# The recurrence's gates and the attention's scores as plain float32 products of 64 partitions

## The chip, the cores and the metric

One program on one NeuronCore of a Trainium2 chip. The metric is the device time of one execution in microseconds (us). The kernel before takes 618.59 us (median of three runs, 617.87 to 619.34); the execution that was profiled took 616.12 us.

## The reference, cut to what matters

One layer of a hybrid backbone over 256 latent tokens and 256 context tokens of width 1024: a conv branch, an attention branch of 8 heads of 64, a recurrence of 8 blocks of 64 in two directions, then a mixture of 16 experts of which each token takes two. The two places that the change touches:

```python
def _block_diag(x, w, bias):                      # the recurrence's gates, 8 blocks of 64 x 64
    xb = x.reshape(bsz, length, RNN_BLOCKS, RNN_BLOCK_W)
    return jnp.einsum("blnk,nkj->blnj", xb, w).reshape(bsz, length, D_RNN) + bias

r = jax.nn.sigmoid(_block_diag(uf, wa, ba))
i = jax.nn.sigmoid(_block_diag(uf, wx, bx))
...
s_loc = jnp.einsum("bqhd,brkhd->bhqrk", qr, kb) * scale    # 64 dims of one head
s_ctx = jnp.einsum("bqhd,bchd->bhqc", qr, kc) * scale
p = jax.nn.softmax(jnp.concatenate([s_loc, s_ctx], axis=-1), axis=-1)
```

## The kernel before

Channels lie on partitions, 128 at a time, tokens along the free axis. Most matrix products are made of three float32r products of a high and a low part (`mm3`, L68 to L70, `gps` and others in the profile): a weight block arrives by DMA in a `raw` tile, ScalarE writes its high part `w` (L73), VectorE the low part (L74), and 24 matmuls of 256 columns use it. `split` (L72) does the same to an operand. This stream of weight blocks runs from 21 us to 362 us: the keys, the conv inputs (54 us on), the recurrence's inputs `rxps` (85 us on), the values, the queries, `rgps`, 24 gate blocks `gps` with 12 branch blocks `bps` between them (177 to 334 us), and the output `ops`. Then the experts run (374 us on), in float32, with weights that DMAs bring.

Beside the stream run generators: the conv's taps and norm in one queue, `rnn(0)`, `rnn(1)` and `attention()` in the other. Each `yield a, b` says how many us of TensorE and of VectorE the step just written takes, and `fill` takes steps from the queues behind each weight block until VectorE's sum has caught up with TensorE's (ScalarE is not in the account). Tile's scheduler then orders each engine's instructions by its own estimate, mostly as they were written.

`rnn(h)` has four units, a pair of 64-channel blocks `b` in a direction `d`. A unit makes `u` (L679, L686), then two full float32 products of 128 partitions, 128 rows out and 512 columns, `pa` (L688) and `px` (L689): their weights `rnnw` hold two 64 x 64 blocks on the diagonal and zeros elsewhere. ScalarE makes `r` of `pa` (L690) and `g` of `px` (L691), then L693 to L695 and VectorE L696 and L697.

`attention()` takes pairs of heads, `b`. The normed keys and queries `qkn` are split into high and low parts: `kz` for the keys of both heads, `qz` for the queries, where each head has a copy of its own with zeros in the other head's 64 partitions (memsets L788 and L789). A score block `sps` of one head and 128 queries is three float32r products of 128 partitions and 512 columns (L804 to L806). Softmax and `values` follow (L808 to L836). `big` has 35 tiles of 512 KB named pieces, which all of these and the first expert weights share; PSUM has four banks for `ax_bank` and four for `mm_bank`.

## Time and profile before

| | us |
|---|---|
| median of three runs (lowest, highest) | 618.59 (617.87, 619.34) |
| profiled execution | 616.12 |
| its span, first to last instruction | 614.3 |
| TensorE busy | 580.2 (94%) |
| VectorE busy | 349.1 (57%) |
| ScalarE busy | 259.8 (42%) |
| GpSimd busy | 19.4 (3%) |
| bytes moved by DMA | 170.65 MB, mean 278 GB/s |

Times in the rows are us from the first instruction, unless they are marked ns. PE is TensorE, PEld its weight loads, DVE VectorE, ACT ScalarE, SP the queue that issues most DMAs. A float32 product shows as two matmul instructions, a float32r one as one. A matmul's end is modelled, so the distance from one start to the next says more than its duration. A share of busy time is a mean over stages that have different limits.

### The profile page before, as it was taken

What the parts mean: (1) busy time and instruction counts of PE and PEld (TensorE: products, weight loads), DVE (VectorE), ACT (ScalarE), POOL (GpSimd) and SP (SyncE); (2) the same over time, 40 slices, a digit from 0 to 9 for tenths busy, and PEclk for the clock granted to TensorE, in tenths of its full rate; (3) what the DMA queues carried; (4) which work ended last, traced back from release to release, by engine and by line L of the source; (5) the groups of instructions that cost most, each with busy time, mean ns of one, the idle gap of its engine ahead of it and who ended that gap; (6) DMA issues with size and microseconds to landing.
All of it is one profiled execution on the core that took longest, in us unless ns stands there. A gap on an engine that the chain in (4) does not pass through costs nothing. (4 is left out here: it accounts for less than half of the span.)

```text
span 614.3 us, 10619 instructions
## 1 busy us (share of the span) xinstructions
PE 580.2 (94%) x4127; PEld 408.1 (66%) x4127; DVE 349.1 (57%) x797; ACT 259.8 (42%) x456; POOL 19.4 (3%) x42
## 2 busy tenths in 40 slices
PE   1899999999999899999999988999999999999986
PEld 0789888778788778888899975335445334454454
DVE  4667899999758968988469554121240314132303
ACT  4345446654598765877545624203012111130101
POOL 0000000000000000103112010000000000000000
PEclk9999999999999999999999999999999999999999
DMA  8983874446853463759969776999999999969961
GB/s 256 367 339 114 310 259 154 137 141 193 278 212 103 138 241 103 236 176 356 313 211 379 283 245 226 388 360 406 402 393 407 407 408 409 398 226 409 409 248 68
DMA packets 51825, 170.65 MB, mean 278 GB/s; under 512 B 5664, under 2 KB 10016, under 8 KB 51744
## 3 DMA queue, kind: packets, MB, share of 16 engines
q1 hardware_dynamic: 46704, 151.26, 67.2%
q0 software_dynamic: 5040, 18.35, 8.6%
q8 instruction: 46, 0.75, 0.5%
q14 instruction: 35, 0.29, 0.1%
HBM read 168.54 MB, written 1.05 MB: 276 GB/s over the span
## 5 line engine op out<-in xcount | busy, mean ns | idle before, releaser
L1162 PE MATMUL ph<-ew,xg 128*64 128x512 f32 (+1 forms) x576 | 115.6, 548 | 3.5 <-PEq L1318 2.8
L73 ACT ACTIVATE w<-raw 128x1024 fp32r<-128x1024 f32 x68 | 71.8, 1056 | 65.6 <-PE gps L69 11.6
L74 DVE TENSOR_TENSOR w<-raw,w 128x1024 fp32r<-128x1024 f32 x68 | 82.9, 1219 | 21.5 <-ACT w L73 20.8
L1162 PEld LDWEIGHTS ph<-ew,xg 128*64 128x64 f32 x576 | 41.5, 137 | 66.0 <-issue 58.3
L70 PE MATMUL gps<-h,w 128*128 128x256 f32 x192 | 55.2, 288 | 1.2 <-DVE w L74 1.2
L68 PE MATMUL gps<-h,w 128*128 128x256 f32 x192 | 56.0, 291 | 0.4 <-DVE y L934 0.4
L69 PE MATMUL gps<-h,w 128*128 128x256 f32 x192 | 54.5, 284 | 0.0
L593 DVE SCALAR_TENSOR_TENSOR cacc<-up,vc,cacc 128x243 f32<-128x243 f32 (+14 forms) x120 | 52.1, 472 | 1.4 <-ACT cacc L585 0.7
L1171 DVE SCALAR_TENSOR_TENSOR he<-sl,gsl,ph 128x256 f32<-128x256 f32 x16 | 7.1, 477 | 77.5 <-PE ph L1162 76.2
L1183 PE MATMUL py<-ew,heT 128*64 128x512 f32 x224 | 49.6, 595 | 1.2 <-ACT heT L1178 0.8
L74 DVE TENSOR_TENSOR ys<-py,ys 128x512 fp32r<-128x512 f32 (+1 forms) x18 | 11.4, 633 | 58.0 <-ACT ys L73 58.0
L68 PEld LDWEIGHTS gps<-h,w 128*128 128x128 f32 x192 | 36.6, 191 | 4.2 <-issue 2.6
L70 PEld LDWEIGHTS gps<-h,w 128*128 128x128 f32 x192 | 36.7, 191 | 2.8 <-issue 1.5
L69 PEld LDWEIGHTS gps<-h,w 128*128 128x128 f32 x192 | 36.7, 191 | 0.9 <-issue 0.7
L1183 PEld LDWEIGHTS py<-ew,heT 128*64 128x64 f32 x224 | 15.5, 137 | 30.8 <-issue 26.0
L1201 DVE SCALAR_TENSOR_TENSOR xl<-scp,g,xl 128x256 f32<-128x256 f32 x72 | 29.2, 475 | 7.5 <-PE scp L1197 7.5
L1167 ACT ACTIVATE sl<-ph 128x512 f32<-128x512 f32 (+1 forms) x9 | 5.0, 550 | 63.1 <-PE ph L1162 40.4
L73 ACT ACTIVATE ys<-py 128x512 fp32r<-128x512 f32 (+1 forms) x18 | 9.9, 550 | 50.5 <-PE py L1183 36.6
L114 POOL DMA_DIRECT2D ew<-in_w_exp x31 | 16.6, 537 | 321.1 <-ACT pp L813 248.8
L1119 ACT ACTIVATE xg<-gps,b2m 128x256 f32<-128x256 f32 x32 | 13.4, 471 | 22.7 <-PE gps L1115 21.8
L349 PE MATMUL mps<-ma,cs 128*32 128x256 f32 (+1 forms) x160 | 10.1, 397 | 13.2 <-DMA ma<-in_mod_a 13.1
L1197 PEld LDWEIGHTS scp<-oT,ys 128*128 128x128 f32 x128 | 15.7, 188 | 6.7 <-issue 5.2
(358 smaller groups left out, 1310.0 us busy)
## 6 DMA issues: line engine op xcount, KB each, us to landing
ew<-in_w_exp SPq DMA_DIRECT2D x161, 512.0 KB, 10.2
raw<-in_w_in SPq DMA_DIRECT2D x40, 512.0 KB, 4.4
ew<-in_w_exp POOLq DMA_DIRECT2D x31, 512.0 KB, 7.3
raw<-in_mod_b SPq DMA_DIRECT2D x28, 512.0 KB, 4.1
ma<-in_mod_a SPq DMA_DIRECT2D x12, 512.0 KB, 10.0
raw<-in_w_br SPq DMA_DIRECT2D x12, 512.0 KB, 4.0
raw<-in_w_out SPq DMA_DIRECT2D x8, 512.0 KB, 7.5
ma<-in_mod_a SPq DMA_DIRECT2D x8, 256.0 KB, 6.7
```

The lines of the kernel that those rows point to most:

```text
L68: pe.matmul(ps, wh, xh, start=start, stop=False, skip_group_check=True)
L69: pe.matmul(ps, wh, xl_, start=False, stop=False, skip_group_check=True)
L70: return pe.matmul(ps, wl, xh, start=False, stop=stop, skip_group_check=True)
L73: act.activation(hi, src, AF.Copy)
L74: dve.tensor_tensor(lo, src, r32(hi), op=ALU.subtract)
L114: queue.dma_start(t, w_exp[6 * p + 2 * i + s, :, 1024 * q:1024 * q + 1024])
L593: dve.scalar_tensor_tensor(cacc[:, b, i0:i1], up[:, b, i0 + o:i1 + o], half_d[:, b * 31 + j:b * 31 + j + 1], cacc[:, b, i0:i1], op0=ALU.mu ...
L1119: act.activation(place(k0 + j), ps[:, j, :], AF.Identity, bias=b2m[:, k0 + j:k0 + j + 1])
L1162: pe.matmul(ph[64 * s:64 * s + 64, cols], xg(k)[:, c:c + 64], w[:, at], start=k == 0 and not h, stop=k == KD - 1, skip_group_check=True)
L1183: pe.matmul(py[q][64 * s:64 * s + 64, :], heT[f // 2][:, f % 2, 64 * s:64 * s + 64], ew[p][2][f][s][:, q * 512:q * 512 + 512], start=f == ...
L1197: pe.matmul(ps[:, j, :], rows_(i, m), toks(m), start=(j == 0 and i == 0), stop=i == parts - 1, skip_group_check=True)
L1201: dve.scalar_tensor_tensor(xl[:, m, :], ps[:, j, :], g2[:, m:m + 1], xl[:, m, :], op0=ALU.mult, op1=ALU.add)
```

## The change

The gates: the two blocks of a unit become two float32 products of 64 partitions each, on partitions 0 to 63 and 64 to 127, each with 128 rows out, of which the first 64 are the one gate and the others the other gate; they go to two banks. The weights lose the zeros and take one piece and one DMA where there were two. ScalarE makes each of `r` and `g` in two instructions of 64 partitions, as the halves lie in two banks. The scores: a pair of heads is two float32 products of 64 partitions, straight from `qkn`, for the same 128 queries, into two banks. `qz` and `kz`, their memsets and splits go, and with them four pieces. A pair of heads is walked by query tile and then head; the planner's costs of the steps are other ones.

```diff
--- before.py
+++ after.py
@@ -660,9 +660,8 @@
     dve.tensor_scalar(ch, ch, -4.0, None, op0=ALU.mult)
     calm.close()
 
-    rnnw = [cut(piece(name="rnnw"), 0, [8, 128]) for _ in range(2)]
-    for d in range(2):
-        load(rnnw[d], rnn_w[:, 8 * d:8 * d + 8, :])
+    rnnw = cut(piece(name="rnnw"), 0, [8, 128])
+    load(rnnw, rnn_w)
     rxp = [cut(piece(name="rxp"), 0, [2, 2, T]) for _ in range(2)]
 
     def rnn(h):
@@ -684,12 +683,16 @@
                 else:
                     out_, in_ = uc[:, :, :T - o], src[:, :, o:]
                 dve.scalar_tensor_tensor(out_, in_, wj, out_, op0=ALU.mult, op1=ALU.add)
-            pa, px = ax_bank(name="pa"), ax_bank(name="px")
-            pe.matmul(pa, rnnw[d][:, 2 * h + b, :], u, start=True, stop=True)
-            pe.matmul(px, rnnw[d][:, 4 + 2 * h + b, :], u, start=True, stop=True)
-            act.activation(r, pa, AF.Tanh, bias=half_r[:, i:i + 1], scale=0.5)
-            act.activation(g, px, AF.Tanh, bias=half_r[:, 8 + i:9 + i], scale=0.5)
-            yield 1.7, 2.0
+
+            pab = [ax_bank(name="pab") for _ in range(2)]
+            for j in range(2):
+                c = slice(64 * j, 64 * j + 64)
+                pe.matmul(pab[j], rnnw[c, 4 * d + 2 * h + b, :], u[c], start=True, stop=True)
+            for o, x, n_ in ((0, r, i), (64, g, 8 + i)):
+                for j in range(2):
+                    c = slice(64 * j, 64 * j + 64)
+                    act.activation(x[c], pab[j][o:o + 64, :], AF.Tanh, bias=half_r[c, n_:n_ + 1], scale=0.5)
+            yield 1.1, 2.0
             act.activation(th, r, AF.Tanh, bias=ch[:, i:i + 1], scale=ch[:, i:i + 1])
             act.activation(r, r, AF.Exp, bias=ch[:, i:i + 1], scale=ch[:, i:i + 1])
             last = act.activation(a2, r, AF.Square)
@@ -780,30 +783,22 @@
             turned.append(tp.rearrange("p t (b c) -> p t b c", b=4)[:, :, :, :2])
         hrstd = rsqrt(turned, 48, 1.0 / HD).rearrange("p (t h) -> p t h", t=6)
         yield 0, 2.5
-        qz = []
-        for i in range(2):
-            t = piece(F32R, "qz")
-            H, L = cut(t, 0, [2, T]), cut(t, 512, [2, T])
-            for x in (H, L):
-                dve.memset(r32(x[64:128, 0, :]), 0.0)
-                dve.memset(r32(x[0:64, 1, :]), 0.0)
-            qz.append((H, L))
-        kz = [piece(F32R, "kz") for _ in range(2)]
         pp = [cut(piece(name="pp"), 0, [2, 512]) for _ in range(2)]
         pts = [cut(piece(name="pt"), 0, [4, T]) for _ in range(4)]
         att_out.extend(cut(piece(F32R, "att"), 0, [4, T]) for _ in range(2))
         oH, oL = att_out
-        yield 0, 1.1
         behind = []
 
-        def scores(b, hh, t):
-            ps = ax_bank(name="sps")
-            q = slice(t * 128, t * 128 + 128)
-            qH, qL = qz[b % 2]
-            kH, kL = kz[b % 2][:, :512], kz[b % 2][:, 512:]
-            pe.matmul(ps, qH[:, hh, q], kH, start=True, stop=False)
-            pe.matmul(ps, qH[:, hh, q], kL, start=False, stop=False)
-            pe.matmul(ps, qL[:, hh, q], kH, start=False, stop=True)
+        def scores(b, t):
+
+            ps = [ax_bank(name="sps") for _ in range(2)]
+            q = 512 + t * 128
+            for hh in range(2):
+                x = qkn[b % 2][64 * hh:64 * hh + 64]
+                pe.matmul(ps[hh], x[:, q:q + 128], x[:, :512], start=True, stop=True)
+            return ps
+
+        def softmax(b, hh, t, ps):
             bias = rpb[b][:, hh, 2 - 2 * t:6 - 2 * t, :].rearrange("p a b -> p (a b)")
             dve.tensor_tensor(ps[:, :T], ps[:, :T], bias, op=ALU.add)
             nm = work.tile([128, 1], F32, tag="nm", name="nm", bufs=4)
@@ -845,24 +840,19 @@
                 pe.transpose(psk[:, t * 128:t * 128 + 128], hx[:, t, :], ident)
             kn = qkn[b % 2][:, :512]
             dve.scalar_tensor_tensor(kn, kb[b], v("kg"), psk, op0=ALU.mult, op1=ALU.mult)
-            kH, kL = kz[b % 2][:, :512], kz[b % 2][:, 512:]
-            split(kH, kL, kn)
-            yield 0.5, 2.3
+            yield 0.5, 1.0
             psq = ax_bank((128, T), "psq")
             for t in range(2):
                 pe.transpose(psq[:, t * 128:t * 128 + 128], hx[:, 4 + t, :], ident)
             qn = qkn[b % 2][:, 512:512 + T]
             dve.scalar_tensor_tensor(qn, qb[:, b, :], qg8, psq, op0=ALU.mult, op1=ALU.mult)
-            qH, qL = qz[b % 2]
-            for hh in range(2):
-                s = slice(64 * hh, 64 * hh + 64)
-                split(qH[s, hh, :], qL[s, hh, :], qn[s, :])
-            yield 0.3, 1.2
+            yield 0.3, 0.5
             pt = pts[2 * (b % 2):2 * (b % 2) + 2]
-            for hh in range(2):
-                for t in range(2):
-                    behind.append((b, hh, t, scores(b, hh, t), pt))
-                    yield 0.7, 1.2
+            for t in range(2):
+                ps = scores(b, t)
+                for hh in range(2):
+                    behind.append((b, hh, t, softmax(b, hh, t, ps[hh]), pt))
+                    yield 1.0 * (1 - hh), 1.2
                     if len(behind) > DEEP:
                         values(*behind.pop(0))
                         yield 0.9, 0.6
@@ -1484,12 +1474,11 @@
     for br in (0, 2, 1):
         order += [CG + br * 8 + m for m in range(8)]
     d["w_in"] = C(np.stack([blk(b).reshape(128, 1024) for b in order]))
-    rw = np.zeros((128, 2, 2, 4, 128), np.float32)
+    rw = np.empty((2, 64, 2, 4, 2, 64), np.float32)
     for gi, a in enumerate((f(rnn_wa)[0], f(rnn_wx)[0])):
-        for n in range(8):
-            s = (n % 2) * 64
-            rw[s:s + 64, :, gi, n // 2, s:s + 64] = a[:, n].transpose(1, 0, 2)
-    d["rnn_w"] = C(rw.reshape(128, 16, 128))
+
+        rw[:, :, :, :, gi] = a.reshape(2, 4, 2, 64, 64).transpose(2, 3, 0, 1, 4)
+    d["rnn_w"] = C(rw.reshape(128, 8, 128))
     col = np.arange(64)
     start = np.clip(col - 8, 0, 48)
     inside = (col[None, :] >= start[:, None]) & (col[None, :] < start[:, None] + 16)
```

## Rows read from the trace of the kernel before

**Rows 1.** The page's first part: busy time, share of the span, instructions

```profile
PE 580.2 (94%) x4127; PEld 408.1 (66%) x4127; DVE 349.1 (57%) x797; ACT 259.8 (42%) x456; POOL 19.4 (3%) x42
```

**Rows 2.** Windows by stage: length, then busy us (instructions) of each engine, clock, DMA

```profile
98.00:133.00 35.00, 35.00 (x207) 26.20 (x204) 34.26 (x69) 21.30 (x30) 0.00 (x0) 1.00 0.44 142
...
165.00:211.00 46.00, 44.53 (x331) 37.70 (x331) 36.43 (x73) 40.72 (x63) 0.00 (x0) 1.00 0.49 162
...
240.00:300.00 60.00, 60.00 (x429) 50.82 (x429) 49.48 (x107) 46.01 (x93) 10.80 (x21) 1.00 0.72 253
...
374.00:614.00 240.00, 228.81 (x1383) 108.62 (x1382) 57.05 (x153) 41.83 (x92) 0.00 (x0) 1.00 0.89 347
```

**Rows 3.** TensorE's waits over the span: us in total, times, longest (two of 21)

```profile
PE pk L1084 <- DVE maskb L1061: 2.8, 1, 2.8
...
PE gps L70 <- DVE w L74: 1.2, 1, 1.2
```

**Rows 4.** TensorE's timeline, first unit of the recurrence: start, length, instruction

```profile
99.09 1.02 PE L689 MATMUL px<-u,rnnw 128*128 128x512 f32 x2
...
100.07 0.28 PE L69 MATMUL rxps<-h,w 128*128 128x256 f32 x1
```

**Rows 5.** TensorE's timeline, one score block between gate matmuls

```profile
245.69 0.40 PE L804 MATMUL sps<-kz,qz 128*128 128x512 f32 x1
...
246.39 0.28 PE L68 MATMUL gps<-h,w 128*128 128x256 f32 x1
246.50 0.28 PE L69 MATMUL gps<-h,w 128*128 128x256 f32 x1
```

**Rows 6.** TensorE's timeline: float32 products of half the columns, two side by side

```profile
400.68 1.89 PE L1162 MATMUL ph<-ew,xg 128*64 128x512 f32 x8
```

**Rows 7.** TensorE's timeline: a visit of two float32 matmuls of a quarter of the columns

```profile
227.40 0.28 PE L70 MATMUL gps<-h,w 128*128 128x256 f32 x1
227.61 1.04 PE L771 MATMUL hps<-qkn,hind 128*32 128x512 f32 x2
...
228.81 0.28 PE L69 MATMUL gps<-h,w 128*128 128x256 f32 x1
```

**Rows 8.** TensorE's timeline: a group cut in two by a gate block's matmuls

```profile
256.70 0.65 PE L833 MATMUL po<-pt,vt 128*64 128x256 f32 x2
...
257.82 1.94 PE L833 MATMUL po<-pt,vt 128*64 128x256 f32 x14
```

**Rows 9.** Groups by line: a gate's activations, 165 to 211 us; busy us, mean ns | idle

```profile
L690 ACT ACTIVATE r<-pa,vc 128x512 f32<-128x512 f32 x4 | 2.7, 683 | 1.0 <-PE pa L688 1.0
```

**Rows 10.** Groups by line, 235 to 300 us: what splits keys, queries and a full tile

```profile
L74 DVE TENSOR_TENSOR qz<-qkn,qz 64x256 fp32r<-64x256 f32 x8 | 3.3, 416 | 0.1
L73 ACT ACTIVATE qz<-qkn 64x256 fp32r<-64x256 f32 x8 | 3.3, 412 | 0.1
...
L74 DVE TENSOR_TENSOR kz<-qkn,kz 128x512 fp32r<-128x512 f32 x4 | 2.7, 687 | 0.0
L73 ACT ACTIVATE kz<-qkn 128x512 fp32r<-128x512 f32 x4 | 2.5, 632 | 2.6 <-DVE qkn L847 2.6
...
L73 ACT ACTIVATE bi<-rgx 128x256 fp32r<-128x256 f32 x4 | 1.4, 408 | 0.0
```

**Rows 11.** ScalarE's timeline in a unit of rnn(1)

```profile
189.76 0.69 ACT L691 ACTIVATE g<-px,vc 128x512 f32<-128x512 f32 x1
190.35 0.71 ACT L610 ACTIVATE sqc<-cacc 128x256 f32<-128x256 f32 x2
```

**Rows 12.** Timeline of VectorE and TensorE: a weight block that comes late

```profile
202.79 1.22 DVE L74 TENSOR_TENSOR w<-raw,w 128x1024 fp32r<-128x1024 f32 x1
...
204.06 0.39 PE L70 MATMUL gps<-h,w 128*128 128x256 f32 x1 [1.15 <-DVE w L74]
```

**Rows 13.** Expert weights: issues on SP (first, last), landing; the last step that uses them

```profile
L114 SPq DMA_DIRECT2D ew<-in_w_exp x161: 327/328/1090, 358.2 to 584.3; - x161
...
DMA to landing us min/median/max: 4.1/10.2/12.7
```

## The prediction

> **What bounds the kernel now.** Read the page's busy shares first: TensorE is busy 580.2 of 614.3 us, and no other engine over 349.1 [rows 1]. Then the windows by stage: from 98 to 133 us, where the first half of the recurrence runs, and from 240 to 300 us, where the attention runs, TensorE is busy for the whole window [rows 2]. Then TensorE's own waits: 2.8 us at the router, and next to nothing in the stages that the change touches, where the longest is 1.2 us for VectorE's low part of a weight block [rows 3]. In the expert stage (374 us on) TensorE is busy 228.8 of 240 us, its list names no wait for an expert weight, and the last one is issued at 584.3 us and lands at most 12.7 us later, 597.0 us, while the span goes on to 614.3 us [rows 2, 3, 13]. Those loads wait for buffers that TensorE frees, so I let the expert stage move as one piece with what comes ahead of it. So TensorE's time in the recurrence and the attention counts one for one, as long as ScalarE and VectorE keep up. They nearly don't in one place: from 165 to 211 us, where rnn(1) runs, ScalarE is busy 40.7 of 46 us, and at 204 us TensorE stood 1.15 us for a weight block whose low part VectorE ended at 204.01 us [rows 2, 12].
>
> **The gates on TensorE.** Before, a unit is four instructions in a row, two for pa and two for px. From px's first start to the second matmul of the weight stream behind it is 100.07 - 99.09 = 0.98 us [rows 4]: two of 0.43 us and one of the stream's 0.12 (246.39 to 246.50) [rows 5]. So a unit is 4 x 0.43 = 1.72 us and pays nothing for the change of type. After, a unit is again four instructions of 512 columns, on two halves of the array's rows. No row of before has row halves. The bounds: they overlap wholly (0.86 us) or not at all (1.72 us). The nearest row is the expert product, with halves of the columns: eight instructions from 400.68 us take 1.89 us, the last one alone about 0.59 (px's pair takes 1.02, less 0.43) [rows 4], so three steps between four pairs take 1.30, 0.43 us for two [rows 6]. I take whole overlap, 0.86 us. The po group shows that two such halves run on their own: 14 instructions of about 0.21 us each in 1.94 us [rows 8].
>
> **The price of a visit.** Going from full to tiled and back isn't free in these rows: from 227.40 to 228.81 is 1.41 us for a gate matmul, two hps of 0.43 and a gate matmul, which should take 0.12 + 0.86 + 0.12 = 1.10; so 0.31 us a visit [rows 7]. The gates and scores of before are full products and pay none [rows 4]. After, each unit and each score pair is a visit. A unit: 0.86 + 0.31 = 1.17 us against 1.72, gain 0.55 us, times 8 units 4.4 us.
>
> **The scores on TensorE.** Before, a block is 246.39 - 245.69 = 0.70 us, a pair of heads 1.40 us [rows 5]. After: 4 float32 instructions, 0.86 + 0.31 = 1.17 us, gain 0.23 us, times 8 pairs 1.8 us. TensorE's sum is 4.4 + 1.8 = 6.2 us. If halves don't overlap at all: units 1.72 + 0.31 against 1.72, scores 2.03 against 1.40, a loss of 8 x 0.31 + 8 x 0.63 = 7.5 us. Between lies a group cut in two, as the schedule did to po [rows 8]: then each half runs alone, 2 x 0.86 + 2 x 0.31 = 2.34 us for 1.17. The pair now needs two free PSUM banks of four at one time, which a score block did not; I take one such cut in sixteen, 1.2 us lost.
>
> **A rule that speaks against it.** The rows of column halves show two in the time of one. The Trainium skill, TensorE: Matmul & The Clock Gate, section "Part 3: Packing small matmuls — row/col tiling", gives for four row tiles 3.07 times the speed of one, not four; no run here shows row tiles. By that share (77%) a pair would take an estimated 1.72 / 1.54 = 1.12 us and not 0.86, and TensorE's sum would fall by 16 x 0.26 = 4.2 to 2.0 us.
>
> **ScalarE.** A gate activation takes 0.69 us, and the next one starts 0.59 us behind it [rows 9, 11]. Half the partitions don't shorten it: the split of 64 partitions takes 412 ns, that of 128 with as many columns 408 [rows 10]. So a unit gets two more of 0.59, 1.18 us, eight units 9.4 us. In rnn(0) ScalarE is busy 21.3 of 35 us [rows 2], and 4 x 1.18 = 4.7 us find room; what it costs if they don't is below. In rnn(1) the 46 us hold 40.7 busy [rows 2], and 4.7 more make 45.4: ScalarE then can't let TensorE through faster than that. So of rnn(1)'s 4 x 0.55 = 2.2 us I count 0.5. What is queued behind the new activations is the high part of the next weight block, and VectorE's low part and TensorE's third product wait for that.
>
> **What goes in the attention.** ScalarE loses the splits, 2.5 + 3.3 = 5.8 us, VectorE 2.7 + 3.3 = 6.0 us and the memsets [rows 10]. TensorE has no idle time there [rows 2], so I cost this at nothing; TensorE's own work is the cover. Four pieces and one weight piece go, and one DMA of 512 KB: loads may start sooner, and nothing waits for a load there [rows 3], so again nothing. The other order of heads and the planner's new costs move steps, not work: the gates ask 1.1 for 1.7 us, close to the 1.17 above.
>
> **The sum.** rnn(0) 4 x 0.55 = 2.2, rnn(1) 0.5, scores 1.8, one cut -1.2: 3.3 us. On the profiled execution 616.12 - 3.3 = 612.8; that one lies 2.5 us under the median, and I put the forecast on the median: 618.6 - 3.3 = 615.3 us, with 613 to 617.3 as its own range.
>
> **Rivals.** Whole gain: the planner spreads rnn(1)'s units so that ScalarE fits, and no group is cut: 618.6 - 6.2 = 612.4 us. For it: ScalarE's load falls from 211 us on. Against: the stand at 204 us. Gain eaten: halves overlap in part, or two or three more groups are cut at 1.2 us each: about 618, between 617.3 and 619.8. On the other side, ScalarE as the bound of the recurrence: if its queue has no room at all, in rnn(0) too, because the four activations of a unit stand ahead of a high part that TensorE is about to need, all of 8 x 1.18 = 9.4 us come on top of TensorE's -6.2: 3.2 us slower, 621.8. It decides from the point at which a weight's high part lands later than TensorE's first use of it; at 204 us that margin is gone already, in rnn(0) the window has 13.7 us free [rows 2]. Last, that the change doesn't do what it says: row halves run one behind the other, 618.6 + 7.5 = 626.1 us.
>
> **How the numbers follow.** Forecast 0.45, whole gain 0.18, eaten 0.17, ScalarE as the bound 0.10, no overlap 0.10. The range reaches from under the whole gain (610.5, if the late weight blocks come sooner as well) to 621.8 and leaves out the last case and the edges. A measurement of this kernel can tell about 0.2%, 1.2 us, from no change: faster takes the first two and a little of the third, 0.65; same most of the third, 0.15; slower the last two, 0.20.
>
> **What would show it.** In the trace of the changed kernel a unit's four matmuls should start in two pairs 0.43 us apart, and the next full matmul some 0.2 us late; four in a row 0.43 us apart would make the overlap wrong. From 165 to 211 us ScalarE should be busy nearly throughout, and TensorE's waits for a low part should grow by 1 to 3 us; no such waits mean the whole gain. In the attention TensorE should stay busy throughout with the experts starting earlier by the whole sum. Expert weights that TensorE waits for would make the last stage's rigid shift wrong.

## The result, and the profile after

The changed kernel takes 636.94 us, median of 4 runs (635.75 to 639.67), beside 618.97 us (617.87 to 620.12) for the kernel before on the same chip: a ratio of 1.0296, with an interval from 1.0258 to 1.0335. It is 18.0 us slower; the forecast was 3.3 us faster, and its range ended at 621.8. The profiled execution is the longest of its runs: 639.67 us, with a span of 637.9 us against 614.3 us before, so the traces below differ by 23.6 us and the medians by 18.0.

The page's first part, as [rows 1]:

```profile
PE 592.3 (93%) x4111; PEld 405.8 (64%) x4111; DVE 343.9 (54%) x777; ACT 270.7 (42%) x462; POOL 19.6 (3%) x42
```

TensorE is busy 12.1 us longer, though the change was to take work from it. That is no contradiction: a matmul counts as busy for as long as it runs, and at half the clock it runs longer (the two pairs of instructions of a score pair start 0.53 us apart at 261.46 us and 0.98 us apart at 270.89 us, where the clock is 0.50). The windows of the changed kernel (length, then busy us and instructions of PE, PEld, DVE, ACT, POOL, then the granted clock, DMA share and GB/s) show where:

```profile
98.00:133.00 35.00, 35.00 (x224) 26.33 (x223) 34.84 (x71) 27.18 (x37) 0.00 (x0) 1.00 0.43 145
165.00:211.00 46.00, 43.75 (x334) 36.10 (x332) 33.02 (x64) 40.58 (x61) 0.00 (x0) 1.00 0.53 174
240.00:258.00 18.00, 18.00 (x116) 12.88 (x115) 7.21 (x16) 9.22 (x18) 1.04 (x2) 1.00 0.63 244
258.00:266.00 8.00, 5.76 (x38) 4.06 (x37) 6.88 (x15) 3.36 (x6) 0.00 (x0) 1.00 0.68 239
266.00:283.00 17.00, 14.33 (x45) 7.26 (x44) 9.42 (x22) 7.05 (x16) 1.42 (x2) 0.51 0.32 94
283.00:300.00 17.00, 15.74 (x97) 10.15 (x95) 13.61 (x34) 13.28 (x30) 3.69 (x7) 0.99 0.43 148
394.00:638.00 244.00, 231.86 (x1385) 109.47 (x1383) 57.27 (x153) 41.84 (x92) 0.00 (x0) 0.99 0.87 340
```

The two windows of the recurrence answer to the first two of [rows 2]: TensorE is as full there as before, ScalarE has 5.9 us more in the first and no more in the second. The stretch from 240 to 300 us, in which TensorE was busy for all 60 us at full clock [rows 2], has come apart. From 240 to 258 us VectorE works 7.2 of 18 us. Then TensorE gets thin (5.76 of 8 us), and from 266 to 283 us its clock is granted at 0.51, the lower of its two levels, 1.2 GHz. No engine is full in those 17 us: VectorE 9.4, ScalarE 7.1. A smaller cut of the same stretch tells what TensorE did ahead of the fall, half busy for 4 us, and that it stayed at 0.50 while it was busy 4.52 of 5 us:

```profile
262.00:266.00 4.00, 1.99 (x11) 0.82 (x8) 3.31 (x8) 2.19 (x5) 0.00 (x0) 1.00 0.36 123
266.00:270.00 4.00, 2.84 (x14) 2.17 (x12) 3.67 (x8) 2.97 (x7) 0.53 (x1) 0.53 0.41 131
270.00:275.00 5.00, 3.98 (x12) 2.11 (x12) 2.97 (x7) 1.73 (x6) 0.89 (x1) 0.50 0.74 211
275.00:280.00 5.00, 4.52 (x12) 1.69 (x14) 2.53 (x7) 1.59 (x4) 0.00 (x0) 0.50 0.01 3
```

TensorE's waits from 205 to 320 us (total us, times, longest), where the kernel before had none over 1.2 us [rows 3]:

```profile
PE gps L70 <- DVE w L74: 3.2, 3, 1.8
PE bps L68 <- ACT bi L73: 2.7, 2, 1.5
PE sps L798 <- DVE qkn L848: 2.3, 2, 1.4
PE ptp L820 <- ACT pp L808: 2.0, 1, 2.0
PE po L828 <- ACT pt L821: 0.9, 2, 0.6
```

Three of these are the attention's own chain: scores wait for queries, the transposes of the softmax for its exponential, the product with the values for the copy of the transposes. In the timeline the first scores start at 261.46 us (241.5 before) and the last at 307.3 (291.6 before), and between 263.4 and 288.4 us no matmul of the stream stands between the attention's steps. Before, gate and branch blocks filled every such gap.

By the starts of the blocks of the stream the 23.6 us come in this way: up to the first gate block 1.9 us less; at the fourth gate block 3.5 us less; by the ninth, behind the first branch block, 2.5 us more; at the fifth branch block 17.4 us more, at the nineteenth gate block 19.3 us more; through the router +0.8, and in the expert stage +3.4.

TensorE's timeline shows the row halves at work, a unit of the recurrence and two pairs of scores:

```profile
99.29 1.13 PE L690 MATMUL pab<-u,rnnw 64*128 64x512 f32 x4
100.35 0.39 PE L68 MATMUL rxps<-h,w 128*128 128x256 f32 x1
100.58 0.28 PE L69 MATMUL rxps<-h,w 128*128 128x256 f32 x1
...
261.46 1.99 PE L798 MATMUL sps<-qkn 64*128 64x512 f32 x8
263.38 0.39 PE L70 MATMUL gps<-h,w 128*128 128x256 f32 x1
```

From a unit's first start to the stream's second matmul are 1.29 us; less one step of the stream, 0.12, that is 1.17 us, the predicted unit. Its four instructions start at 99.294, 99.300, 99.827 and 99.834 us: two side by side, then two more. Eight score instructions, two pairs in one visit, take 263.38 - 261.46 = 1.92 us.

### The profile page after: what moved, and what is told of

Same layout as the page of the kernel before. It is cut to its first block, busy times and chain, and to the rows that moved or that the text cites. A ratio compares the mean times of both kernels' runs of the same rounds, so it can differ in the third digit from the quotient of the medians.

```text
span 637.9 us, 10583 instructions
## 1 busy us (share of the span) xinstructions
PE 592.3 (93%) x4111; PEld 405.8 (64%) x4111; DVE 343.9 (54%) x777; ACT 270.7 (42%) x462; POOL 19.6 (3%) x42
## 5 line engine op out<-in xcount | busy, mean ns | idle before, releaser
L1152 PE MATMUL ph<-ew,xg 128*64 128x512 f32 (+1 forms) x576 | 118.2, 560 | 4.0 <-PEq L1308 4.0
L593 DVE SCALAR_TENSOR_TENSOR cacc<-up,vc,cacc 128x241 f32<-128x241 f32 (+14 forms) x120 | 51.7, 474 | 1.2 <-ACT cacc L585 0.7
L74 DVE TENSOR_TENSOR ys<-py,ys 128x512 fp32r<-128x512 f32 (+1 forms) x18 | 11.4, 633 | 58.0 <-ACT ys L73 58.0
L1109 ACT ACTIVATE xg<-gps,b2m 128x256 f32<-128x256 f32 x32 | 13.4, 471 | 21.6 <-PE gps L1105 20.7
L68 PE MATMUL bps<-bi,w 128*128 128x256 f32 x64 | 18.5, 293 | 2.7 <-ACT bi L73 2.7
```

The source lines that it names most:

```text
L68: pe.matmul(ps, wh, xh, start=start, stop=False, skip_group_check=True)
L74: dve.tensor_tensor(lo, src, r32(hi), op=ALU.subtract)
L593: dve.scalar_tensor_tensor(cacc[:, b, i0:i1], up[:, b, i0 + o:i1 + o], half_d[:, b * 31 + j:b * 31 + j + 1], cacc[:, b, i0:i1], op0=ALU.mu ...
L1109: act.activation(place(k0 + j), ps[:, j, :], AF.Identity, bias=b2m[:, k0 + j:k0 + j + 1])
L1152: pe.matmul(ph[64 * s:64 * s + 64, cols], xg(k)[:, c:c + 64], w[:, at], start=k == 0 and not h, stop=k == KD - 1, skip_group_check=True)
```

## The experiments

The change has two kinds of edits: work (gates, scores, splits) and the numbers that the generators give to the planner. Fourteen kernels were run. In the table "first scores" is the start of the first score matmul; "gate blocks" is the time from the start of the first gate block to that of the 22nd, less the 133.7 us of before, and "experts" that from the first expert product to the end, less the 240.4 us of before, both read from the timeline of one profiled execution each. Between executions whose instructions stand in the same order, starts at the first gate block differ by up to 2.8 us, so a difference of a microsecond or two in one of these columns says nothing by itself. The trace of before is that of the shortest of its executions on record (616.12 us, with a mean granted clock of 0.999; most others have 0.994 to 0.997), so differences to it, experts' column included, lean to plus by some 3 to 4 us over a whole span.

| kernel | us, median (lowest to highest) | interval of the ratio to before | first scores | gate blocks | experts |
|---|---|---|---|---|---|
| after | 636.94 (635.75 to 639.67) | 1.0258 to 1.0335 | 261.5 | +21.2 | +3.3 |
| x1_costs_alone | 634.52 (633.62 to 636.03) | 1.0168 to 1.0297 | 258.8 | +16.3 | +0.9 |
| x2_work_alone | 624.99 (623.05 to 627.96) | 1.0059 to 1.0117 | 247.6 | +6.5 | -0.4 |
| x3_gate_cost | 630.71 (629.48 to 633.46) | 1.0118 to 1.0245 | 245.8 | +11.4 | +3.1 |
| x4_att_costs | 636.01 (635.20 to 636.85) | 1.0192 to 1.0320 | 259.9 | +15.4 | +7.1 |
| y1_halved_acts | 626.96 (625.39 to 630.92) | 1.0103 to 1.0190 | 247.0 | +4.9 | +1.7 |
| y2_gates_alone | 626.60 (626.14 to 628.04) | 1.0099 to 1.0148 | 246.1 | +5.3 | +5.9 |
| y3_scores_alone | 626.96 (626.32 to 629.06) | 1.0109 to 1.0163 | 243.4 | +0.3 | +7.1 |
| y4_gate_cost_alone | 632.59 (630.25 to 634.46) | 1.0181 to 1.0257 | 256.7 | +12.5 | +3.6 |
| w1_gates_diagonal | 627.09 (624.74 to 628.80) | 1.0079 to 1.0144 | 246.7 | +3.1 | +4.4 |
| z1_scores_padded | 629.60 (627.79 to 631.67) | 1.0117 to 1.0195 | 242.8 | +4.9 | +6.4 |
| z2_sixteen_more | 623.28 (621.03 to 626.24) | 1.0036 to 1.0083 | 241.8 | +1.6 | +4.0 |
| z3_gate_cost_up | 625.44 (624.88 to 626.70) | 1.0051 to 1.0119 | 234.9 | +1.9 | +4.4 |
| w2_sqrt_last | 622.10 (618.75 to 625.82) | 1.0002 to 1.0060 | 243.1 | -0.9 | +3.6 |
| z4_sixteen_late | 625.12 (624.34 to 627.45) | 1.0046 to 1.0108 | 244.3 | 0.0 | +5.9 |

The kernel before took 618.97 to 620.18 us (medians) beside them.

### Work or the planner's costs: six kernels

**x1_costs_alone.** The kernel before, its work untouched, with the numbers of after:

```diff
-            yield 1.7, 2.0
+            yield 1.1, 2.0
...
-        yield 0, 1.1
...
-            yield 0.5, 2.3
+            yield 0.5, 1.0
...
-            yield 0.3, 1.2
+            yield 0.3, 0.5
...
-                    yield 0.7, 1.2
+                    yield 1.0 * (1 - t), 1.2
```

> The kernel before with its own products, splits and zeros; only the planner's costs are those of the changed kernel (gates 1.1 for 1.7, keys 0.5/1.0, queries 0.3/0.5, the zeros' step gone, scores 1.0 for each second block). Theory, the planner: the cheaper costs start the attention about four jobs later and write it between half as many weight blocks, so TensorE stands on the softmax's chain; this kernel then shows it as well, 632 to 648 us, with the whole attention between few gate blocks and a stretch at the lower clock. Rival, the products: the time is lost in the row halves, their activations or their pairs of banks; then this kernel stays at 617 to 620 us.

Measured: 634.52 us. **x2_work_alone** is the reverse, after with 1.7 for the gates and, in the attention, the numbers of before (a pair of scores asks 1.4 us of TensorE, two blocks of 0.7).

> The changed kernel with the costs of before told to the planner (1.7 for the gates, 2.3 and 1.2 for keys and queries, the step of 1.1 kept, 1.4 for a pair of scores). Theory, the planner: the loss goes and TensorE's own gain is left, 612 to 617 us. Rival, the products: 632 to 638 us.

Measured: 624.99 us, in neither range. So the numbers alone cost 634.5 - 619.4 = 15.1 us and the work alone 5.6 us; their sum, 20.7, is near the 18.0 of both. In x1 TensorE waits in the attention, from 205 to 320 us, and the clock falls as in after:

```profile
PE sps L803 <- ACT qz L73: 4.6, 3, 2.4
PE ptp L824 <- DVE ri L814: 3.9, 1, 3.9
...
266.00:283.00 17.00, 14.36 (x64) 10.06 (x63) 10.93 (x25) 10.01 (x21) 1.59 (x3) 0.67 0.20 63
```

In x2, with the same work as after but the old numbers, the same window is full:

```profile
266.00:283.00 17.00, 16.98 (x124) 12.97 (x121) 13.28 (x29) 11.98 (x25) 2.12 (x4) 1.00 0.57 195
```

**x3_gate_cost** is after with the gates' number alone back at 1.7, **x4_att_costs** after with the attention's numbers alone back:

> The changed kernel with only the gates' cost put back to 1.7. Theory, the planner: the attention begins as early as before but is written between some seven blocks in place of twelve; part of the loss stays, 620 to 630 us. Rival, the late start alone (the recurrence taking more blocks): 612 to 618 us. Rival, the products: 632 to 638 us.

> The changed kernel with only the attention's costs put back. Theory, the planner's density: the attention starts as late as in the changed kernel but is spread over eleven blocks, so 612 to 620 us. Rival, the late start alone: 630 us or more. Rival, the products: 632 to 638 us.

Measured: 630.71 and 636.01 us. The gates' number is the larger part: putting it back gains 6.2 us, putting the others back 0.9 us; once it is back, the others are worth 630.71 - 624.99 = 5.7 us more. In the gate blocks the two are less unequal, 9.8 and 5.8 us of after's +21.2; x4 loses again in the expert stage (+7.1 for +3.3) what it gains there. x3 comes out just above its first theory's range. x4's first theory fell: a late start with old costs, spread over eleven blocks, costs what the rival of the late start said (the products' 632 to 638 us, which fits too, is ruled out by x2).

**y4_gate_cost_alone** is the kernel before with `yield 1.1, 2.0` for `yield 1.7, 2.0` and nothing else.

> The kernel before, all its work, with only the gates' cost told as 1.1. Theory, the late start: the recurrence spreads over more blocks and the attention begins late, so a good part of the costs' 15 us is here, 624 to 632 us. Rival, only the attention's own costs matter: 617 to 621 us.

Measured: 632.59 us, 13.5 us more, for one number in a line that makes no instruction. Its account explains the late start. A unit's two yields add 2.0 + 1.7 of VectorE and 1.7 of TensorE, 2.0 net; with 1.1 they add 2.6 net. So fewer units fit beside each weight block, the recurrence reaches further along the stream, and the attention, which stands behind it in the same queue, starts later: its first scores at 256.7 us, not 241.5. The number was near the truth of TensorE (a unit does take 1.17 us), and worse for the order: the account has no ScalarE and no clock in it.

Why the late start costs 13.5 us is shown only in part. Going through the account by hand gives some twelve blocks of the stream with steps of the attention before, and six or seven in after and x1; but for y4 and x4 it gives eleven, so fewer blocks can't be the cause there. What the traces of after, x1 and y4 have in common is one long stretch without a matmul of the stream, ahead of the fifth branch block: 25.0 us in after (263.4 to 288.4), 29.5 in x1, 13.4 in y4 (256.2 to 269.6). The longest from 205 to 320 us is 6.3 us in before, 6.1 in x2 and x3 and 6.7 in x4. Why a late start alone leads there, and where x3 and x4 lose theirs, stays open.

**z3_gate_cost_up** goes the other way, 2.4 for 1.7.

> The kernel before with one number changed: a gate unit asks the planner for 2.4 us of cover, not 1.7 (1.1 gave 632.59). The attention then starts three or four blocks of the stream earlier and is spread as widely as before. Theory 1: what cost time at 1.1 is the attention pressed into few blocks, where TensorE waits for the softmax; at 2.4 TensorE is as full there as before, and the time is 618 to 621, with the attention's first scores 8 us earlier or more. Theory 2: any move of the planner from its tuned place costs; 624 or more.

Measured: 625.44 us, in the range of theory 2, so neither direction of that number gains. The attention starts earlier (234.9 us) and TensorE's waits from 215 to 325 us come to 0.4 us, as the first theory wanted; but rnn(1) is now pressed together ahead of it, and there TensorE stands 3.5 us for a weight's high part on ScalarE (up to 206.1 us) and 2.0 us for a low part on VectorE. At the nineteenth gate block z3 is 5.2 us late. My 618 to 621 was too low: I had looked at the attention and not at what the same number does to the recurrence. Its 4.4 us in the expert stage are of the kind told of below.

### The gates' work: ScalarE, tables, or the tiling

**y1_halved_acts** leaves the products of before and only cuts each gate activation in two of 64 partitions:

```diff
-            act.activation(r, pa, AF.Tanh, bias=half_r[:, i:i + 1], scale=0.5)
-            act.activation(g, px, AF.Tanh, bias=half_r[:, 8 + i:9 + i], scale=0.5)
+            for x, ps, n_ in ((r, pa, i), (g, px, 8 + i)):
+                for j in range(2):
+                    c = slice(64 * j, 64 * j + 64)
+                    act.activation(x[c], ps[c, :], AF.Tanh, bias=half_r[c, n_:n_ + 1], scale=0.5)
```

> The kernel before, its products and its costs, with each of the gates' two activations cut into two of 64 partitions, so that ScalarE alone gets the changed kernel's work. Theory, ScalarE: what is left of the loss with the old costs (625.0 against 619.4) is ScalarE's, so this is 622 to 627 us, TensorE standing at the first branch block for ScalarE. Rival, TensorE's visits and banks: 617 to 621 us.

**y2_gates_alone** has the whole change of the gates (row halves and four activations) with the number 1.7:

> The kernel before with the gates' change alone, at the old cost of 1.7. Theory, ScalarE: the gates carry the loss that is left, 621 to 627 us. Rival, the scores carry it: 614 to 618 us.

Measured: 626.96 and 626.60 us. The two more activations of a unit cost as much alone as with the products that were to pay for them. In both, TensorE stands 2.3 us ahead of the first branch block, where before it stood 0.3. This is TensorE's list of y1, 160 to 240 us:

```profile
PE bps L68 <- ACT b2r L905: 2.3, 1, 2.3
```

The list puts it down to `b2r`, the short activation that ScalarE ends at nearly the same time. What fits in all kernels looked at is the high part `w` of the block's own weight: TensorE starts 0.05 us after it ends. In ScalarE's queue it stands behind the last quarter of the convolution's output, `bi`, and a square root. First before, then y1:

```profile
207.81 0.40 ACT L73 ACTIVATE bi<-cacc 128x256 fp32r<-128x256 f32 x1
209.07 1.04 ACT L73 ACTIVATE w<-raw 128x1024 fp32r<-128x1024 f32 x1
210.16 0.38 PE L68 MATMUL bps<-bi,w 128*128 128x256 f32 x1 [0.32 <-ACT b2r L903]
...
212.47 0.40 ACT L73 ACTIVATE bi<-cacc 128x256 fp32r<-128x256 f32 x1
213.72 1.04 ACT L73 ACTIVATE w<-raw 128x1024 fp32r<-128x1024 f32 x1
214.81 0.38 PE L68 MATMUL bps<-bi,w 128*128 128x256 f32 x1 [2.27 <-ACT b2r L905]
```

4.7 us late: half of the 8 x 1.18 = 9.4 us that eight units add to ScalarE. In the kernel before, the weight's high part was ready at 210.11 us and the block started at 210.16: the slack that the forecast wanted to spend wasn't there.

**w1_gates_diagonal** was to take ScalarE's part away. Each row half writes its own column half, so that r and g still come out as full tiles of 128 partitions:

```diff
-                pe.matmul(pab[j], rnnw[c, 4 * d + 2 * h + b, :], u[c], start=True, stop=True)
...
+            pa, px = ax_bank(name="pa"), ax_bank(name="px")
+            for gi, ps in enumerate((pa, px)):
+                for j in range(2):
+                    c = slice(64 * j, 64 * j + 64)
+                    pe.matmul(ps[c], rnnw[c, 4 * d + 2 * h + b, 64 * gi:64 * gi + 64], u[c], start=True, stop=True)
+            act.activation(r, pa, AF.Tanh, bias=half_r[:, i:i + 1], scale=0.5)
+            act.activation(g, px, AF.Tanh, bias=half_r[:, 8 + i:9 + i], scale=0.5)
```

> The kernel before with the gates alone changed, in another form: the two halves of the rows also write two halves of the columns, so that a unit's r products go to one bank and its i products to another, each over all 128 partitions, and ScalarE keeps its two activations of 128 partitions a unit, not four. Scores, planner's costs (1.7) and order of work as before. Theory 1, ScalarE: what the changed gates lose between the third and the eighth gate block (+4.6 to +6.1 us in the three kernels that had four activations) is the two more activations a unit. Then that loss goes, TensorE's saving of 8 x 0.45 us shows, and the time is 615 to 617. Theory 2, the visits: the loss is the change of TensorE's tiling itself, which makes the weight stream behind it late; then it stays, and the time is 624 to 627, as with the gates alone changed (626.6).

Measured: 627.09 us. The form takes away more than ScalarE's part: a unit is now four products, eight instructions on quarters of the array. This is its first unit and the stream's second matmul behind it:

```profile
97.99 1.08 PE L690 MATMUL pa<-u,rnnw 64*64 64x512 f32 x4
...
100.08 0.28 PE L69 MATMUL rxps<-h,w 128*128 128x256 f32 x1
```

2.09 us less one step of the stream, 0.12, are 1.97 us a unit, where after has 1.17 and before, counted in the same way, 1.72 to 1.82. So w1 saves TensorE nothing, and the 8 x 0.45 us of its expectation were never there. Taken by the number, the theory of ScalarE fell; the timeline of ScalarE says why it needn't have:

```profile
208.16 1.28 ACT L703 ACT_TABLE_LOAD   x1
209.45 1.06 ACT L703 ACTIVATE th<-th 128x1024 f32<-128x1024 f32 x1
210.53 1.28 ACT L622 ACT_TABLE_LOAD   x1
211.82 0.42 ACT L622 ACTIVATE thc<-cacc 128x256 f32<-128x256 f32 x1
212.25 1.28 ACT L703 ACT_TABLE_LOAD   x1
213.55 1.06 ACT L703 ACTIVATE th<-th 128x1024 f32<-128x1024 f32 x1
214.51 0.40 ACT L73 ACTIVATE bi<-cacc 128x256 fp32r<-128x256 f32 x1
```

The scheduler, with other times to go by, has put the convolution's last tanh between the two square roots of rnn(1). Each change of function in these rows loads a table, 1.28 us; `bi` comes at 214.5 us and the weight's high part at 215.86. Behind TensorE's stand of 3.4 us its clock falls as well:

```profile
212.00:222.00 10.00, 5.79 (x26) 5.04 (x25) 9.93 (x16) 6.34 (x10) 0.00 (x0) 0.62 0.24 77
```

(w1, after, x4 and z3 have 12 table loads, the others 10; in after it is the tanh of a gate block that stands between the two square roots.) **w2_sqrt_last** holds the square roots of rnn(1) behind that tanh:

```diff
-        with tc.issue_after(last.ins):
+        with tc.issue_after(last.ins), tc.issue_after((pins or [last])[-1].ins):
```

> The kernel with the gates on diagonal quarters (two activations a unit), and with the square roots of rnn(1) held back behind the last tanh of the convolution, so that ScalarE's table isn't changed to and fro between them (12 table loads in that kernel, 10 before). Theory 1, the last quarter of the convolution: TensorE's stand ahead of the first branch block ends when that quarter and the weight's high part come out of ScalarE's queue, and two of the 3.4 us stood there are the two table loads; with them gone, that block starts 2 to 4 us earlier than 215.9 us, and the stage loses at most 3 us to before, not 5.3; the time is 621 to 625, as what comes behind the router falls. Theory 2, the tiling: the changed gates make TensorE late themselves; the block starts at 215 us or later, and the time is 625 to 628.

Measured: 622.10 us. In its timeline ScalarE goes from the tanh to one table load and then on:

```profile
210.20 0.40 ACT L624 ACTIVATE thc<-cacc 128x256 f32<-128x256 f32 x1
210.62 1.28 ACT L705 ACT_TABLE_LOAD   x1
211.91 1.06 ACT L705 ACTIVATE th<-th 128x1024 f32<-128x1024 f32 x1
212.88 0.40 ACT L73 ACTIVATE bi<-cacc 128x256 fp32r<-128x256 f32 x1
```

The first branch block starts at 210.3 us, as before, not at 215.9 as in w1, as the weight's high part is now ready at 210.30 us, ahead of that tanh. Only two of its matmuls stand there: 22 matmuls of a gate block follow, and the rest from 213.3 us, when `bi` is there. The gate blocks take 0.9 us less than before, which is within what executions differ by. So the tiling makes nothing late by itself, and the extra time of w1 was that queue and the low clock behind it. What the row halves' gain is worth w2 can't tell: its units take 1.96 us on TensorE, like w1's, and no kernel has a unit of 1.17 us without the two more activations. The pin by itself, on the kernel before, was not run.

### The scores' work

**y3_scores_alone** has the scores' change with the numbers of before for the attention:

> The kernel before with the scores' change alone, at the attention's old costs. Theory, ScalarE: the scores give a little, 616 to 619 us. Rival, the scores carry the loss by their pairs of banks: 621 to 626 us.

Measured: 626.96 us, 7.9 us more and above both ranges, and nothing of it in the gate blocks (+0.3). In their stage the scores show neither a gain nor a loss that stands out of the noise. In the traces 7.1 us arise in the expert stage, which the edit does not touch. The two halves of the work don't add up for the same reason: the gates alone lose 7.5 us (y2), the scores alone 7.9, both together 5.6 (x2), with +5.9, +7.1 and -0.4 us in the expert stage. The trace of y3 has 4.0 of its 7.1 us as stands of TensorE in the middle of expert products, with a lower clock behind them (0.66 from 500 to 505 us and from 595 to 600; before has 1.00 in both). This is y3's list from 372 to 640 us:

```profile
PE ph L1151 <- PEq L1307: 4.2, 2, 4.0
PE ph L1151 <- issue: 3.4, 2, 2.7
```

Before had 2.8 and 0.8 us in these two lines. Expert weights were there: counted in the order of their loads, they land at least 5 us ahead of their first use in every kernel. "PEq" is TensorE's own sequencer, "issue" is time in which nothing that the profile shows was waited for.

### A stage that no edit touches: three kernels

The experts have branches, taken by counts that come out of the router. If TensorE's code has to be loaded at such a place, the time could hang on where the code lies, and any matmul more or less ahead of it would shift that. **z1_scores_padded** is y3 with 32 matmuls of 4 columns put ahead of the score products, which are overwritten by them, so that the program has as many matmuls as before:

```diff
+                for _ in range(2):
+                    pe.matmul(ps[hh][:, :4], x[:, q:q + 128], x[:, :4], start=True, stop=True)
                 pe.matmul(ps[hh], x[:, q:q + 128], x[:, :512], start=True, stop=True)
```

> The scores' change alone (626.96 before, with 32 matmul instructions fewer in TensorE's program) with 32 matmuls of 4 columns put ahead of the score products, in the same banks, so that TensorE's program has as many matmuls as before. Theory 1, the place of the code: the 7.1 us that the scores' change lost in the expert stage, which it doesn't touch, hang on where the experts' branches lie in TensorE's program; with the count as before the expert stage is within 1.5 us of before, and the time is 619 to 621 (the small ones cost about 1 us). Theory 2, the work: the loss hangs on the attention's other order of heads, what it leaves to load and where the loads stand; then it stays, 626 to 629.

Measured: 629.60 us; the expert stage stays long (+6.4), and theory 1 fell. The same number of matmuls doesn't bring the old time back. **z2_sixteen_more** is the kernel before with one more matmul of 32 columns ahead of each score block, overwritten like those of z1:

```diff
+            pe.matmul(ps[:, :32], qH[:, hh, q], kH[:, :32], start=True, stop=True)
             pe.matmul(ps, qH[:, hh, q], kH, start=True, stop=False)
```

> The kernel before with 16 matmuls of 32 columns more, one ahead of each block of scores, and nothing else. They take under 0.1 us each, 0.5 to 1.5 us in all. Theory 1, the place of the code: the expert stage, untouched, can become 3 to 7 us longer by the shift alone; 622 to 627. Theory 2, the work: the expert stage stays within 1 us of before, and the time is 619.5 to 621.

Measured: 623.28 us, 3.9 us more; in the traces, 6.6 us apart, 4.0 us are in the expert stage. To have the place of the code without any change in the order of work, **z4_sixteen_late** puts sixteen such matmuls behind the attention, two ahead of each output block; every other instruction of every engine keeps its order, but for a few of one output block's own matmuls:

```diff
         ps = mm_bank((128, T), "ops")
+        for _ in range(2):
+            pe.matmul(ps[:, :32], wh[:, :128], yH(0)[:, :32], start=True, stop=True)
```

> The kernel before with 16 matmuls of 32 columns more, two ahead of each of the eight output blocks, behind the attention and ahead of the router; every other instruction of every engine stands in its order. They take 16 x 0.1 us at most. Theory 1, the place of the code: the expert stage, whose work, order and weights are those of before, starts at most 2 us later and becomes 2 to 6 us longer, with stands of TensorE in which a load of instructions lands; the time is 621 to 626. Theory 2: without a change of order ahead of it the expert stage keeps its length within 1 us, and the time is 619 to 621; then the growth with sixteen early ones came from the order of work.

Measured: 625.12 us, 4.9 us more. The traces are 11.3 us apart: 2.9 us arise ahead of the edit, 2.5 from there to the first expert product (the expectation had at most 2 for its start), and 5.9 in the expert stage. z2 and z4 stand at the same instructions, inside the gather's products `gps` of the experts (L1115 before). TensorE's timeline there, before, then z2, then z4:

```profile
542.40 3.67 PE L1115 MATMUL gps<-oh,hT 128*128 128x256 f32 x29 [0.85 <-PEq L1318]
...
545.34 0.83 PE L1116 MATMUL gps<-oh,hT 128*128 128x256 f32 x5 [0.88 <-PEq L1319]
548.12 0.51 PE L1116 MATMUL gps<-oh,hT 128*128 128x256 f32 x2 [1.95 <-issue]
...
548.82 0.72 PE L1117 MATMUL gps<-oh,hT 128*128 128x256 f32 x4 [1.16 <-ACT sl L1169]
551.61 0.59 PE L1117 MATMUL gps<-oh,hT 128*128 128x256 f32 x2 [2.06 <-issue]
```

Before, 29 matmuls follow one another; in z2 and z4 TensorE stops for 2 us after the fifth and the fourth. The queues that load instructions move packets in that very stretch (z4, 546.9 to 551.9 us: packets, MB, share):

```profile
q14 instruction: 3, 0.02, 2.8%
q8 instruction: 1, 0.02, 1.5%
```

and the granted clock falls behind the stop, here z4 (0.84; z2 has 0.92) and then before, 540 to 562 us:

```profile
540.00:562.00 22.00, 18.36 (x112) 11.47 (x105) 5.10 (x13) 5.37 (x13) 0.00 (x0) 0.84 0.68 241
...
540.00:562.00 22.00, 20.72 (x122) 11.05 (x120) 7.68 (x19) 5.97 (x14) 0.00 (x0) 1.00 0.87 318
```

z2 and z4 show that sixteen tiny matmuls ahead of the expert stage make the kernel 4 to 5 us slower and that stage 4 to 6 us longer, in z4 without another order of work. Of z4's 5.9 us, 22 us at a clock of 0.84 make an estimated 3.5 at most, and the stop about 2. That the cause is where TensorE's code lies is the reading that fits, and is not shown: the stage also starts later, and no kernel shifts the one without the other. That the stop is a load of instructions is what the rows fit, not more: in the expert stages of the sixteen traces (the router's own left out) TensorE has 43 places with more than 1.4 us from one matmul's start to the next's, and at all 43 a packet of an instruction queue is under way in between, while a stretch of 1.7 us picked at random there meets one in about 37% of cases; but most packets land without a stand. And the stops of z2 and z4 come four or five matmuls behind the branch, not at it, so which load it would be stays open. The Trainium skill, Runtime: NRT & Kernel Launch, section "Instruction fetch mechanics", says that instructions are fetched ahead in sequence and that a taken branch whose target is out of the window has to wait for a fetch; the 43 stands of the expert stage, 1.4 to 4.7 us each from start to start, are of a kind with it, though no run here shows the window. In w2 one such stand takes 4.14 us; that w2 would be the faster kernel without it (its median lies 1.92 us behind before) is not shown:

```profile
547.24 0.59 PE L1118 MATMUL gps<-oh,hT 128*128 128x256 f32 x3 [4.14 <-issue]
```

## Why the prediction was wrong, step by step

**What bounds the kernel.** That TensorE is full in the stages of [rows 2] was read rightly, but it was read as a property of the stage. It is one of the order of work: TensorE is full because the planner spreads the chains over enough weight blocks. And full didn't mean free of a second limit: at the first branch block the weight's high part left ScalarE 0.05 us before TensorE used it, so whatever TensorE gained ahead of 210 us had to be waited out there.

**The overlap, the visit, the unit.** Right. Two row halves in float32 run side by side; a unit takes 1.17 us, as predicted (its two pairs of instructions start 0.53 us apart, not 0.43, with less of the visit's price behind them). The 3.07 times that the Trainium skill, TensorE: Matmul & The Clock Gate, section "Part 3: Packing small matmuls — row/col tiling", gives for four row tiles made a pair an estimated 1.12 us without the visit's price. The rows don't bear that estimate out for two halves: two pairs of scores in one visit average 0.96 us with the visit's price.

**What that is worth.** Sized at 2.2 us in rnn(0), 0.5 in rnn(1) and 1.8 in the scores. At the fourth gate block after stood 3.5 us ahead, of the size of those sums but within what single executions differ by; it gave that back by the first branch block. What the gates' gain would be worth with nothing else in the way is not shown: y2, which has it, stands for ScalarE as y1 does, and w1 and w2 don't have it (1.97 us a unit). Of the scores' gain none shows (y3). The cut group, priced at one in sixteen, came three times in after's sixteen, each time in a score pair, and once in x2 and in y3.

**ScalarE.** The mechanism was right, the size and the place were off. Four activations were priced at 1.18 us a unit, and I let that cost 1.7 us of gain in rnn(1). It costs 4.9 us in the gate blocks by itself (y1). I looked at how much of a 46 us window ScalarE was busy; what counted was one result at its end, the first branch block's weight, that came 4.7 us late. The rival "ScalarE as the bound" had the cost at 9.4 us, about twice that, and its place (a high part that TensorE needs) was right.

**"The other order of heads and the planner's new costs move steps, not work", costed at nothing.** This is the step that failed, and it carries most of the error: 15.1 us for the numbers alone (x1), 13.5 for one of them (y4). They move steps, and that was the price: the attention started 15 to 20 us later, in after and x1 with about half as many blocks to hide behind, and TensorE went 13 to 30 us without a matmul of the stream (after, x1, y4). I compared 1.1 with the true 1.17 us of a unit and took a truer number for a harmless one, without going through the account to see when the attention would start. The late start and the fewer blocks could have been worked out from the code alone; what y4 loses with eleven blocks could not, as far as these runs tell.

**What goes in the attention.** "TensorE's own work is the cover" held only while gate and branch blocks stood between the attention's steps. Alone, the attention is a chain of scores, maximum, exponential, transposes and copies in which no engine is full, and TensorE's clock falls to 0.51 besides. How the 17 to 20 us divide between the waits and the clock was not told apart, as no kernel kept the clock up in that stretch; 17 us at 0.51 make an estimate of 8.3 us at most for the clock itself, under half of after's 21.2 in the gate blocks.

**The expert stage as one piece.** Wrong: -0.4 to +7.1 us in kernels that don't touch it. Its weights were in time, as said; TensorE's own code, the reading that fits, was not on the list.

**The range.** No rival led to 637. The dearest, 626.1 us, was that the halves don't overlap, which they do. The rivals all asked what an instruction costs; none asked what the numbers in the planner do.

## What to carry to other kernels

Where a planner interleaves chains by declared costs, a change of a cost is a change of the schedule: go through its account and find when each chain starts and how many blocks it gets, before pricing any instruction. An operation that saves time on the full engine pays only if the next joint, here the last input of the first branch block, has slack; look for it in the trace and see what two more instructions on another engine do to that one result. About one per cent can come and go in a stage that the edit doesn't touch, here one with branches, so a gain of that size needs the untouched stages looked at one by one. And a kernel that is to take one cause away should be checked in its trace for what else it takes away: w1 gave up the saving that it was to show.

## What the hardware showed beyond that

TensorE's clock was granted at 0.50 to 0.53 from 266 us on, after 4 us in which TensorE was busy 1.99 us, the longest wait there being 2.0 us, and it stayed so while TensorE was busy 4.52 of 5 us. A table load on ScalarE takes 1.28 us and the next activation starts right behind it (208.16 + 1.28 to 209.45 us in w1); the Trainium skill, ScalarE: Activation LUTs, section "What ACT_TABLE_LOAD costs", gives 1283 ns, with which the rows agree, and about 1380 ns more for a drain at each switch, which these rows don't show.
